# RoPE on one NeuronCore: whole batch rows in bf16, cast inside GpSimd-queue DMAs

## The chip, the core and the metric

The kernel runs on one NeuronCore of a Trainium2 chip. The metric is the device time of one execution in microseconds (us). Before the change the median of 10 executions is 318.76 us (318.5 to 323.6).

The core has engines that work side by side: VectorE (DVE in the profile), ScalarE (ACT), GpSimd (POOL), TensorE (PE, not used here) and SyncE (SP, used here only to issue transfers). Data lie in DRAM and are moved by 16 DMA engines into SBUF, which has 128 partitions, and back. A transfer is issued on the queue of the engine that issues it: SP's, ACT's or POOL's.

## The reference

Rotary position embedding on interleaved pairs: in each head, elements 2i and 2i+1 form a pair, which is rotated by an angle that depends on the position in the sequence and on i.

```python
x  # (8, 2048, 16, 64) float32: batch, position, head, element of the head
cos, sin  # (2048, 32) float32
x1, x2 = x_pairs[..., 0], x_pairs[..., 1]
out1 = x1 * cos - x2 * sin
out2 = x1 * sin + x2 * cos
out = np.stack([out1, out2], axis=-1)  # back to (8, 2048, 16, 64), float32
```

x has 67.1 MB and so has the output. The two tables have 0.26 MB each.

## The kernel before

One position is 16 heads x 64 elements = 1024 float32, 4 KB. The kernel cuts the sequence into G = 2 halves of 1024 positions; in each half a partition holds K = 8 consecutive positions. A tile `xt` is one half of one batch: 128 partitions x 8 positions, 32 KB a partition, 4 MB, and contiguous in DRAM in rows of 32 KB. There are 16 such tiles, and NX = 5 buffers for them.

A tile is worked on in pieces of 4 positions (4096 elements a partition). The first tile is cut into 1, 1, 2 and 4 positions, the last into 4, 2, 1 and 1, so that work begins and ends on small pieces. For each piece:

- `halve` (L75): ScalarE casts the piece from float32 to a bf16 buffer `xh`, of which there are three.
- `rotate`: VectorE does three tensor_tensor instructions in bf16. L94 multiplies by the sine table into `qt`, L95 multiplies in place by the cosine table, and L100 adds `qt` with the elements of each pair swapped. The swap is a matter of addressing. The sign of the first sine of each pair is put into the table.
- `widen` (L105): ScalarE casts the result back to float32, over the tile's own place. Then ACT's queue gets the store (L109): one for a tile, four for the last tile. After a tile's last piece SP's queue gets the load of the tile five further on (L70), which takes the same buffer and waits for its store.

The order is written out by hand (`manual_schedule`). SP issues the first tile's four pieces, the two tables (L115, L116), then four more tiles. VectorE makes bf16 tables from the float32 ones (L121 to L123). In the loop over pieces, ScalarE casts the next piece in before VectorE rotates this one, and then casts this one out.

Of the kernel before, what the change touches and what calls it, by code (L numbers as in the profile page):

```python
# [2 lines left out]

# [4 lines left out]


@with_exitstack  # L10
def kernel(
    ctx: ExitStack,
    tc: tile.TileContext,
    x: bass.AP,
    cos: bass.AP,
    sin: bass.AP,
    out: bass.AP,
):
    nc = tc.nc
    fp32 = mybir.dt.float32  # L20
    bf16 = mybir.dt.bfloat16
    mult = mybir.AluOpType.mult
    add = mybir.AluOpType.add

    B, S, H, D = x.shape
    P = 128
    K = 8
    G = S // (P * K)
    D2 = D // 2
    HD = H * D  # L30
    NX = 5


    x_t = x.rearrange("b (g p k) h d -> b g p k (h d)", p=P, k=K)
    out_t = out.rearrange("b (g p k) h d -> b g p k (h d)", p=P, k=K)
    cos_t = cos.rearrange("(g p k) c -> p g (k c)", p=P, k=K)
    sin_t = sin.rearrange("(g p k) c -> p g (k c)", p=P, k=K)

    consts = ctx.enter_context(tc.tile_pool(name="consts", bufs=1))
    xpool = ctx.enter_context(tc.tile_pool(name="xpool", bufs=NX))  # L40
    hpool = ctx.enter_context(tc.tile_pool(name="hpool", bufs=1))

    cos_sb = consts.tile([P, G, K * D2], fp32)
    sin_sb = consts.tile([P, G, K * D2], fp32)
    c_tab = consts.tile([P, G, K, D], bf16)
    s_tab = consts.tile([P, G, K, D], bf16)

    groups = [(g, b) for g in range(G) for b in range(B)]
    n = len(groups)
    first_runs = [(0, 1), (1, 2), (2, 4), (4, 8)]  # L50
    last_runs = [(0, 4), (4, 6), (6, 7), (7, 8)]

    def load_runs(i):
        return first_runs if i == 0 else last_runs if i == n - 1 else [(0, K)]

    def store_runs(i):
        return last_runs if i == n - 1 else [(0, K)]


    pieces = []  # L60
    for i in range(n):
        runs = first_runs if i == 0 else last_runs if i == n - 1 else [(0, 4), (4, 8)]
        pieces += [(i, k0, k1) for k0, k1 in runs]
    tiles, halved, rotated = {}, {}, {}

    def load(i):
        g, b = groups[i]
        tiles[i] = xpool.tile([P, K, HD], fp32, name="xt")
        for k0, k1 in load_runs(i):
            nc.sync.dma_start(out=tiles[i][:, k0:k1], in_=x_t[b, g, :, k0:k1])  # L70

    def halve(j):
        i, k0, k1 = pieces[j]
        halved[j] = hpool.tile([P, 4, HD], bf16, name="xh", bufs=3)
        nc.scalar.copy(out=halved[j][:, : k1 - k0], in_=tiles[i][:, k0:k1])  # L75

    def rotate(j):
        i, k0, k1 = pieces[j]
        g, _ = groups[i]
        nk = k1 - k0  # L80
        xh = halved.pop(j)
        qt = hpool.tile([P, 4, HD], bf16, name="qt")

        def rows(a):
            return a[:, :nk].rearrange("p k (h e) -> p k h e", h=H, e=D)

        def tab(a):
            return dataclasses.replace(
                a,
                offset=a.offset + (g * K + k0) * D,  # L90
                ap=[a.ap[0], [D, nk], [0, H], [1, D]],
            )

        nc.vector.tensor_tensor(out=rows(qt), in0=rows(xh), in1=tab(s_tab), op=mult)  # L94
        nc.vector.tensor_tensor(out=rows(xh), in0=rows(xh), in1=tab(c_tab), op=mult)  # L95
        q_swap = dataclasses.replace(
            qt, offset=qt.offset + 1, ap=[qt.ap[0], [2, nk * HD // 2], [-1, 2]]
        )
        xh3 = xh[:, :nk].rearrange("p k (a j) -> p (k a) j", j=2)
        nc.vector.tensor_tensor(out=xh3, in0=xh3, in1=q_swap, op=add)  # L100
        rotated[j] = xh

    def widen(j):
        i, k0, k1 = pieces[j]
        nc.scalar.copy(out=tiles[i][:, k0:k1], in_=rotated.pop(j)[:, : k1 - k0])  # L105
        g, b = groups[i]
        for r0, r1 in store_runs(i):
            if r1 == k1:
                nc.scalar.dma_start(out=out_t[b, g, :, r0:r1], in_=tiles[i][:, r0:r1])  # L109
        if k1 == K and i + NX < n:  # L110
            load(i + NX)

    with tc.manual_schedule():
        load(0)
        nc.sync.dma_start(out=cos_sb, in_=cos_t)  # L115
        nc.sync.dma_start(out=sin_sb, in_=sin_t)  # L116
        for i in range(1, NX):
            load(i)
        s2 = s_tab.rearrange("p g k (i j) -> p (g k i) j", j=2)
        sin_flat = sin_sb.rearrange("p g c -> p (g c)")  # L120
        nc.vector.tensor_copy(out=s2[:, :, 0], in_=sin_flat)  # L121
        nc.vector.tensor_scalar_mul(s2[:, :, 1], sin_flat, -1.0)  # L122
        nc.vector.tensor_copy(  # L123
            out=c_tab.rearrange("p g k (i j) -> p (g k i) j", j=2),
            in_=cos_sb.rearrange("p g c -> p (g c)").to_broadcast([P, G * K * D2, 2]),
        )
        halve(0)
        for j in range(len(pieces)):
            if j + 1 < len(pieces):
                halve(j + 1)  # L130
            rotate(j)
            widen(j)


# [1 line left out]
_INS = ['x', 'cos', 'sin']  # L136
_OUTS = [((8, 2048, 16, 64), 'float32')]


# [23 lines left out]
```

## Time and profile before

| | us |
|---|---|
| median of 10 executions | 318.76 |
| the profiled execution | 318.48 |
| its span in the trace | 316.7 |
| ScalarE, 30 casts in of 128x4096, each | 3.604 |
| ScalarE, 30 casts out of 128x4096, each | 3.602 |
| VectorE, 90 tensor_tensor of 128x4096, each | 2.292 |
| VectorE, tensor_tensor of 128x1024, each | 0.69 |
| median time from issue to landing, 4 MB load | 26.6 |
| median time from issue to landing, 4 MB store | 38.3 |

The span runs from the first to the last thing in the trace; 1.8 us of the profiled execution lie outside of it. An engine's busy time is the sum of its instructions; issuing a DMA does not count. The time from issue to landing contains the time in which a transfer stood behind others. The DMA row of the slices shows how busy the 16 DMA engines were on average, in tenths, and the row below it what they moved.

### The profile page before, as it was taken

The page shows a single profiled execution, that of the slowest core. Times are in us where ns is not written, and L with a number is a line of the kernel's source. Part 1 is how long each engine was busy: PE and PEld are TensorE (multiplying, and loading weights), DVE is VectorE, ACT ScalarE, POOL GpSimd, SP SyncE. Part 2 cuts the span into 40 slices and gives each one's busy share as a digit, 9 for nine tenths or more (in the row PEclk, how much of TensorE's full clock was granted, in tenths as well). Part 3 has the DMA queues.
Part 4 walks back from the last instruction along what each step waited for, and adds up shares of the span by engine and source line. Part 5 has one row for each costly group of instructions (what it writes and reads, how often), then busy time and mean ns, then how long its engine had stood idle before and what let it go on. Part 6 is the DMA issues. An engine that isn't in the chain of part 4 may idle for free.

```text
span 316.7 us, 352 instructions
## 1 busy us (share of the span) xinstructions
DVE 223.2 (70%) x111; ACT 230.0 (73%) x73; POOL 0.2 (0%) x4
## 2 busy tenths in 40 slices
DVE  0189999999999596693957939488440999999112
ACT  4078899999998693976949679495804999997322
POOL 0000000000000000000000000000000000000000
DMA  7999999999999999999999999999999999999997
GB/s 306 422 464 397 464 397 435 426 455 406 464 397 464 397 460 406 455 426 436 447 414 455 410 455 406 455 406 459 410 451 439 422 426 430 424 430 445 442 414 302
DMA packets 6450, 134.76 MB, mean 426 GB/s; under 512 B 688, under 2 KB 1200, under 8 KB 1968
## 3 DMA queue, kind: packets, MB, share of 16 engines
q1 hardware_dynamic: 3712, 67.63, 50.0%
q10 hardware_dynamic: 2736, 67.11, 49.1%
q14 instruction: 2, 0.02, 0.0%
HBM read 67.63 MB, written 67.11 MB: 425 GB/s over the span
## 4 chain that ended last, share of the span: by engine, by line
DMA 72%; ACT 16%; DVE 4%; issue 3%; another core or an unknown queue 2%; SPq 1%; ACTq 0%
DMA out_dram<-xt 38%; DMA xt<-in_x_dram 31%; ACT xt L105 9%; ACT xh L75 7%; DMA sin_sb<-in_sin_dram 4%; DVE xh L95 1%; DVE xh L100 1%; DVE qt L94 1%; SPq L70 1%; ACTq L109 0%; DVE s_tab L121 0%; SPq L115 0%; DVE s_tab L122 0%; DVE c_tab L123 0%
## 5 line engine op out<-in xcount | busy, mean ns | idle before, releaser
L75 ACT CAST xh<-xt 128x4096 bf16<-128x4096 f32 (+2 forms) x36 | 116.1, 3224 | 66.7 <-DMA xt<-in_x_dram 61.3
L105 ACT CAST xt<-xh 128x4096 f32<-128x4096 bf16 (+2 forms) x36 | 116.0, 3223 | 14.7 <-DVE xh L100 14.4
L94 DVE TENSOR_TENSOR qt<-xh,s_tab 128x4096 bf16<-128x4096 bf16 (+2 forms) x36 | 74.0, 2055 | 70.9 <-ACT xh L75 70.0
L95 DVE TENSOR_TENSOR xh<-xh,c_tab 128x4096 bf16<-128x4096 bf16 (+2 forms) x36 | 74.0, 2055 | 1.2
L100 DVE TENSOR_TENSOR xh<-xh,qt 128x4096 bf16<-128x4096 bf16 (+2 forms) x36 | 74.0, 2055 | 1.2
L121 DVE CAST s_tab<-sin_sb 128x512 bf16<-128x512 f32 x1 | 0.5, 453 | 14.5 <-DMA sin_sb<-in_sin_dram 14.5
L75 ACT ACT_TABLE_LOAD x1 | 1.3, 1283 | 0.7 <-PEq L147 0.7
L123 DVE CAST c_tab<-cos_sb 128x1024 bf16<-128x1024 f32 x1 | 0.7, 683 | 0.0
L122 DVE TENSOR_SCALAR s_tab<-sin_sb 128x512 bf16<-128x512 f32 x1 | 0.4, 441 | 0.0
L147 POOL MEMSET const-bfloat16-1.0<- 128x1 bf16 x1 | 0.1, 102 | 0.0
L147 POOL MEMSET const-uint8-127<- 128x1 uint8 x1 | 0.1, 102 | 0.0
L147 POOL MEMSET const-float32-0.0<- 128x1 f32 x1 | 0.1, 99 | 0.2 <-issue 0.2
L147 POOL MEMSET const-float32-1.0<- 128x1 f32 x1 | 0.1, 99 | 0.0
## 6 DMA issues: line engine op xcount, KB each, us to landing
out_dram<-xt ACTq DMA_DIRECT2D x15, 4096.0 KB, 38.3
xt<-in_x_dram SPq DMA_DIRECT2D x14, 4096.0 KB, 26.6
xt<-in_x_dram SPq DMA_DIRECT2D x2, 2048.0 KB, 16.4
xt<-in_x_dram SPq DMA_DIRECT2D x4, 512.0 KB, 24.2
xt<-in_x_dram SPq DMA_DIRECT2D x2, 1024.0 KB, 20.0
out_dram<-xt ACTq DMA_DIRECT2D x1, 2048.0 KB, 17.6
out_dram<-xt ACTq DMA_DIRECT2D x1, 1024.0 KB, 11.7
out_dram<-xt ACTq DMA_DIRECT2D x2, 512.0 KB, 4.1
```

Source lines behind the costliest of these rows:

```text
L70: nc.sync.dma_start(out=tiles[i][:, k0:k1], in_=x_t[b, g, :, k0:k1])
L75: nc.scalar.copy(out=halved[j][:, : k1 - k0], in_=tiles[i][:, k0:k1])
L94: nc.vector.tensor_tensor(out=rows(qt), in0=rows(xh), in1=tab(s_tab), op=mult)
L95: nc.vector.tensor_tensor(out=rows(xh), in0=rows(xh), in1=tab(c_tab), op=mult)
L100: nc.vector.tensor_tensor(out=xh3, in0=xh3, in1=q_swap, op=add)
L105: nc.scalar.copy(out=tiles[i][:, k0:k1], in_=rotated.pop(j)[:, : k1 - k0])
L121: nc.vector.tensor_copy(out=s2[:, :, 0], in_=sin_flat)
L122: nc.vector.tensor_scalar_mul(s2[:, :, 1], sin_flat, -1.0)
L123: nc.vector.tensor_copy(out=c_tab.rearrange("p g k (i j) -> p (g k i) j", j=2), in_=cos_sb.rearrange("p g c -> p (g c)").to_broadcast([P, ...
L147: nc = _bacc.Bacc("TRN2", target_bir_lowering=False, num_devices=1)
```

## The change

A tile becomes a whole batch row: 128 partitions x 16 positions. It lies in SBUF as bf16 (32 KB a partition), and in DRAM as rows of 64 KB. There are 8 tiles and again 5 buffers. The cast is part of the transfer: loads (L56) and stores (L59) are issued on GpSimd's queue with float32 on one side and bf16 on the other.

The first two positions of the first tile (1 MB) come in float32 through SP's queue into a staging tile (L85), and ScalarE casts them (L91). The last four positions of the last tile (2 MB) are cast by ScalarE into the same staging tile and go out in float32 through SP's queue (L121). A copy of one element (L119), which writes into the tile before the last, stands ahead of that cast and waits until that tile has been stored.

VectorE works in place in the tile, on 8 positions at a time (8192 elements a partition), in the first tile on 2, 6 and 8. These are 17 pieces of three instructions.

GpSimd's queue has this order: load 0 (14 positions), load 1, the store of the first two positions once they are rotated, loads 2, 3 and 4, the store of the rest of tile 0, store 1, load 5, store 2, load 6, store 3, load 7, stores 4, 5 and 6, and the store of the first twelve positions of tile 7. Loads 5, 6 and 7 wait until the tile whose buffer they take has been stored. A store waits for VectorE's work on its positions.

```diff
--- before.py
+++ after.py
@@ -24,112 +24,101 @@
     B, S, H, D = x.shape
     P = 128
-    K = 8
-    G = S // (P * K)
+    K = S // P
+    KP = 8
     D2 = D // 2
     HD = H * D
     NX = 5
+    HEAD = 2
+    TAIL = 4
-    x_t = x.rearrange("b (g p k) h d -> b g p k (h d)", p=P, k=K)
-    out_t = out.rearrange("b (g p k) h d -> b g p k (h d)", p=P, k=K)
-    cos_t = cos.rearrange("(g p k) c -> p g (k c)", p=P, k=K)
-    sin_t = sin.rearrange("(g p k) c -> p g (k c)", p=P, k=K)
+    x_t = x.rearrange("b (p k) h d -> b p k (h d)", p=P, k=K)
+    out_t = out.rearrange("b (p k) h d -> b p k (h d)", p=P, k=K)
+    cos_t = cos.rearrange("(p k) c -> p (k c)", p=P, k=K)
+    sin_t = sin.rearrange("(p k) c -> p (k c)", p=P, k=K)
     consts = ctx.enter_context(tc.tile_pool(name="consts", bufs=1))
     xpool = ctx.enter_context(tc.tile_pool(name="xpool", bufs=NX))
-    hpool = ctx.enter_context(tc.tile_pool(name="hpool", bufs=1))
+    qpool = ctx.enter_context(tc.tile_pool(name="qpool", bufs=1))
+    stage = ctx.enter_context(tc.tile_pool(name="stage", bufs=1))
-    cos_sb = consts.tile([P, G, K * D2], fp32)
-    sin_sb = consts.tile([P, G, K * D2], fp32)
-    c_tab = consts.tile([P, G, K, D], bf16)
-    s_tab = consts.tile([P, G, K, D], bf16)
+    cos_sb = consts.tile([P, K * D2], fp32)
+    sin_sb = consts.tile([P, K * D2], fp32)
+    c_tab = consts.tile([P, K, D], bf16)
+    s_tab = consts.tile([P, K, D], bf16)
-    groups = [(g, b) for g in range(G) for b in range(B)]
-    n = len(groups)
-    first_runs = [(0, 1), (1, 2), (2, 4), (4, 8)]
-    last_runs = [(0, 4), (4, 6), (6, 7), (7, 8)]
+    tiles = {}
-    def load_runs(i):
-        return first_runs if i == 0 else last_runs if i == n - 1 else [(0, K)]
+    def load(b, k0=0):
+        if b not in tiles:
+            tiles[b] = xpool.tile([P, K, HD], bf16, name="xt")
+        nc.gpsimd.dma_start(out=tiles[b][:, k0:], in_=x_t[b, :, k0:])
-    def store_runs(i):
-        return last_runs if i == n - 1 else [(0, K)]
+    def store(b, k0=0, k1=K):
+        nc.gpsimd.dma_start(out=out_t[b, :, k0:k1], in_=tiles[b][:, k0:k1])
-    pieces = []
-    for i in range(n):
-        runs = first_runs if i == 0 else last_runs if i == n - 1 else [(0, 4), (4, 8)]
-        pieces += [(i, k0, k1) for k0, k1 in runs]
-    tiles, halved, rotated = {}, {}, {}
-    def load(i):
-        g, b = groups[i]
-        tiles[i] = xpool.tile([P, K, HD], fp32, name="xt")
-        for k0, k1 in load_runs(i):
-            nc.sync.dma_start(out=tiles[i][:, k0:k1], in_=x_t[b, g, :, k0:k1])
-    def halve(j):
-        i, k0, k1 = pieces[j]
-        halved[j] = hpool.tile([P, 4, HD], bf16, name="xh", bufs=3)
-        nc.scalar.copy(out=halved[j][:, : k1 - k0], in_=tiles[i][:, k0:k1])
-    def rotate(j):
-        i, k0, k1 = pieces[j]
-        g, _ = groups[i]
+    def rotate(b, k0, k1):
         nk = k1 - k0
-        xh = halved.pop(j)
-        qt = hpool.tile([P, 4, HD], bf16, name="qt")
+        xp = tiles[b][:, k0:k1]
+        qt = qpool.tile([P, KP, HD], bf16, name="qt")
         def rows(a):
-            return a[:, :nk].rearrange("p k (h e) -> p k h e", h=H, e=D)
+            return a.rearrange("p k (h e) -> p k h e", h=H, e=D)
         def tab(a):
             return dataclasses.replace(
-                a,
-                offset=a.offset + (g * K + k0) * D,
-                ap=[a.ap[0], [D, nk], [0, H], [1, D]],
+                a, offset=a.offset + k0 * D, ap=[a.ap[0], [D, nk], [0, H], [1, D]]
             )
-        nc.vector.tensor_tensor(out=rows(qt), in0=rows(xh), in1=tab(s_tab), op=mult)
-        nc.vector.tensor_tensor(out=rows(xh), in0=rows(xh), in1=tab(c_tab), op=mult)
+        nc.vector.tensor_tensor(out=rows(qt[:, :nk]), in0=rows(xp), in1=tab(s_tab), op=mult)
+        nc.vector.tensor_tensor(out=rows(xp), in0=rows(xp), in1=tab(c_tab), op=mult)
         q_swap = dataclasses.replace(
             qt, offset=qt.offset + 1, ap=[qt.ap[0], [2, nk * HD // 2], [-1, 2]]
         )
-        xh3 = xh[:, :nk].rearrange("p k (a j) -> p (k a) j", j=2)
-        nc.vector.tensor_tensor(out=xh3, in0=xh3, in1=q_swap, op=add)
-        rotated[j] = xh
-    def widen(j):
-        i, k0, k1 = pieces[j]
-        nc.scalar.copy(out=tiles[i][:, k0:k1], in_=rotated.pop(j)[:, : k1 - k0])
-        g, b = groups[i]
-        for r0, r1 in store_runs(i):
-            if r1 == k1:
-                nc.scalar.dma_start(out=out_t[b, g, :, r0:r1], in_=tiles[i][:, r0:r1])
-        if k1 == K and i + NX < n:
-            load(i + NX)
+        x3 = xp.rearrange("p k (a j) -> p (k a) j", j=2)
+        nc.vector.tensor_tensor(out=x3, in0=x3, in1=q_swap, op=add)
     with tc.manual_schedule():
-        load(0)
+        head = stage.tile([P, TAIL, HD], fp32, name="st")
+        for k in range(HEAD):
+            nc.sync.dma_start(out=head[:, k : k + 1], in_=x_t[0, :, k : k + 1])
         nc.sync.dma_start(out=cos_sb, in_=cos_t)
         nc.sync.dma_start(out=sin_sb, in_=sin_t)
-        for i in range(1, NX):
-            load(i)
-        s2 = s_tab.rearrange("p g k (i j) -> p (g k i) j", j=2)
-        sin_flat = sin_sb.rearrange("p g c -> p (g c)")
-        nc.vector.tensor_copy(out=s2[:, :, 0], in_=sin_flat)
-        nc.vector.tensor_scalar_mul(s2[:, :, 1], sin_flat, -1.0)
+        load(0, HEAD)
+        load(1)
+        nc.scalar.copy(out=tiles[0][:, :HEAD], in_=head[:, :HEAD])
+        s2 = s_tab.rearrange("p k (i j) -> p (k i) j", j=2)
+        nc.vector.tensor_copy(out=s2[:, :, 0], in_=sin_sb)
+        nc.vector.tensor_scalar_mul(s2[:, :, 1], sin_sb, -1.0)
         nc.vector.tensor_copy(
-            out=c_tab.rearrange("p g k (i j) -> p (g k i) j", j=2),
-            in_=cos_sb.rearrange("p g c -> p (g c)").to_broadcast([P, G * K * D2, 2]),
+            out=c_tab.rearrange("p k (i j) -> p (k i) j", j=2),
+            in_=cos_sb.to_broadcast([P, K * D2, 2]),
         )
-        halve(0)
-        for j in range(len(pieces)):
-            if j + 1 < len(pieces):
-                halve(j + 1)
-            rotate(j)
-            widen(j)
+        for b in range(B):
+            if b == 0:
+                rotate(b, 0, HEAD)
+                store(b, 0, HEAD)
+                for c in range(2, NX):
+                    load(c)
+                rotate(b, HEAD, KP)
+            for k0 in range(KP if b == 0 else 0, K, KP):
+                rotate(b, k0, k0 + KP)
+            if b < B - 1:
+                store(b, HEAD if b == 0 else 0)
+            if b >= 1 and b - 1 + NX < B:
+                load(b - 1 + NX)
+        store(B - 1, 0, K - TAIL)
+        tail = stage.tile([P, TAIL, HD], fp32, name="st")
+        nc.scalar.copy(out=tiles[B - 2][:1, 0, :1], in_=tiles[B - 1][:1, K - 1, :1])
+        nc.scalar.copy(out=tail, in_=tiles[B - 1][:, K - TAIL :])
+        nc.sync.dma_start(out=out_t[B - 1, :, K - TAIL :], in_=tail)
 # ---- launch: one core; inputs and outputs as the reference has them ----
```

## The prediction

> **What bounds the kernel now.** I read the page's engine shares and its slices first, then the queue list, then the windows query for the rate stage by stage, and last the timeline of the end.
>
> ```profile
> span 316.7 us, 352 instructions
> DVE 223.2 (70%) x111; ACT 230.0 (73%) x73; POOL 0.2 (0%) x4
> DMA  7999999999999999999999999999999999999997
> DMA packets 6450, 134.76 MB, mean 426 GB/s; under 512 B 688, under 2 KB 1200, under 8 KB 1968
> q1 hardware_dynamic: 3712, 67.63, 50.0%
> q10 hardware_dynamic: 2736, 67.11, 49.1%
> ```
>
> Neither compute engine reaches three quarters of the span, and the DMA row is full in every slice but the first and the last. The loads (q1) and the stores (q10) together take 99.1% of sixteen engines' time. So the bound is bytes through the DMA engines, and a stage is worth what it adds to those bytes or to the gaps between them. The windows, with columns span, DVE, ACT, POOL, clock, DMA share and GB/s:
>
> ```profile
> 0.00:3.00 3.00, 0.00 (x0) 1.28 (x1) 0.20 (x4) 1.00 0.36 91
> 24.00:30.00 6.00, 5.25 (x3) 6.00 (x3) 0.00 (x0) 1.00 1.01 437
> 40.00:60.00 20.00, 18.90 (x9) 19.54 (x7) 0.00 (x0) 1.00 0.97 419
> 120.00:160.00 40.00, 28.08 (x13) 28.70 (x9) 0.00 (x0) 1.00 1.00 433
> 302.00:306.00 4.00, 0.00 (x0) 0.00 (x0) 0.00 (x0) 1.00 0.85 361
> 314.00:316.70 2.70, 0.00 (x0) 0.00 (x0) 0.00 (x0) 1.00 0.26 106
> ```
>
> From 24 to 30 us only loads run (the first store is issued at 36 us): 437 GB/s. From 120 to 160 us loads and stores share the engines: 433. That mixing opposite directions brings nothing says that an engine has one budget for both. At the start 3.00 us x (1 - 91/437) = 2.4 us are lost, at the end 2.70 x (1 - 106/433) = 2.0 us; the dips at 40 to 60 us (14/433 x 20 = 0.6) and 302 to 306 us (72/433 x 4 = 0.7) are what else a better order could save.
>
> How two queues share an engine is seen at the end, where the last load comes in one-position pieces (4 KB rows) beside stores with rows of 32 and 16 KB:
>
> ```profile
> 298.78 1.04 ACT L75 CAST xh<-xt 128x1024 bf16<-128x1024 f32 x1 [5.53 <-DMA xt<-in_x_dram]
> 307.88 1.04 ACT L75 CAST xh<-xt 128x1024 bf16<-128x1024 f32 x1 [6.26 <-DMA xt<-in_x_dram]
> ```
>
> The last 0.52 MB needs 9.1 us, 58 GB/s of some 430: the queue with short rows gets about one row per row of the other queue, not half of the bytes.
>
> **What the Trainium skill says.** "DMA: Bandwidth & Descriptors", section "SWDGE vs HWDGE vs iDMA": a cast during a transfer has to be issued from GpSimd, whose cores write the descriptors into rings in SBUF. The trace of before has no such transfer. Same page, "Queues, rings and completion order": each engine goes round its queues packet by packet; the 58 GB/s above agrees. Same page, "Latency and other measured facts": engines 7 and 15 are usually slower, with the GpSimd queue's rings as its best guess at the cause; before uses only hardware queues, so no run here shows it. "SBUF — State Buffer", section "Who interferes with whom": tensor_tensor takes the shared read interface only, so it should not hold up descriptor writing (the page calls this inferred); not shown here either.
>
> **The change part by part.**
>
> *The two casts on ScalarE go.* 36 + 36 casts, 116.1 + 116.0 us of ACT. What stays is one head cast of 2048 elements (1.90 us, the same shape's row), a table load of 1.28, a one-element copy and a tail cast of 4096 (3.60): about 7 us. On the path they were worth nothing except at the ends, since the DMA never ran dry in the middle.
>
> *VectorE.* Rows of 1024, 2048 and 4096 elements take 692, 1226 and 2292 ns, so 0.52 ns an element more; 8192 elements come to 2292 + 4096 x 0.52 = 4424 ns, 6144 to 3358. Fourteen pieces of eight positions, 14 x 3 x 4.424 = 185.8; one of six, 10.1; one of two, 3.7; the table instructions 1.6: sum 201.2 us against 223.2. These 22 us lie beside the DMA. Cover: tile b is rotated 26.5 us after tile b-1. With load 0 landed at about 22 us, tiles 0, 2, 4 and 7 are done near 45, 98, 151 and 231 us (tile 7 needs its load, below). At 19.4 us a tile (8.39 MB at 433) the queue reaches their stores near 104, 162, 240 and 300 us. More than 50 us of slack; VectorE would have to be a quarter slower to matter.
>
> *Queue order on GpSimd.* One queue carries load 0 (14 positions), load 1, store of the first two positions, loads 2 to 4, store 0, store 1, load 5, store 2, load 6, store 3, load 7, stores 4 to 7. A load waits for the store of the tile whose buffer it takes, and everything later on GpSimd waits behind it. Each time the store just issued is still to move 19.4 us of data, against a completion latency of some 2 us (last issue at 312.2, end at 316.7 for 0.5 MB), so I charge nothing; if that cover were gone, it would cost a gap of 2 to 3 us for each of the three waiting loads. The first store is different: loads 2 to 4 stand behind it, and it waits for VectorE. Loads 0 and 1 with head and tables are 17.3 MB, ending near 2.4 + 39.6 = 42 us; if the tables land before about 35 us, nothing is lost. See the rivals.
>
> *Bytes.* 67.11 MB in and 67.11 MB out on the DRAM side are unchanged, tables 0.52: 134.74 MB. On the SBUF side bf16 halves them for all but 3.1 MB. Which side the engine's time follows is not shown in before, since all its transfers are as wide on both sides. Bounds: the wide side, 0% gain; the narrow side, half of the time. I take the wide side: a load still has to bring in four bytes an element and a store to send out four, and since a mixture of directions gained nothing over one, I see no idle half that a narrower far side would free.
>
> *The rate of the casting queue.* Bounds: 437 (nothing lost, the loads-only window) and, for loss, no limit by any reason in the profile. The nearest price is the skill's own table for GpSimd-issued loads, same DMA page, section "Bandwidth", "Measured", which lists 425 GB/s for 16 MB; I use its rate column alone. I take 425 for the loads and this trace's 433 for the stores, for which there is no such figure.
>
> Sum: GpSimd loads 66.06 MB / 425 = 155.4 us. All else, 68.68 MB / 433 = 158.6. Start 2.4 (SP's first issue comes at 0.73 us as before). End 2.0. Two queues finishing within a row of each other at the end, and the switch into the software queue: 0.5, an estimate from the dips of 0.6 and 0.7 above. Span 318.9. The profiled execution took 318.48 with a span of 316.7, so 1.8 lie around it, and the median of the ten runs is 0.3 above that execution: 318.9 + 1.8 + 0.3 = 321.0.
>
> *The tail.* The one-element copy on ScalarE waits for the store of tile 6, then the 3.6 us cast, then SP issues 2.1 MB with 16 KB rows. At that time about 6 us of the 14.5 us of the GpSimd store (48 KB rows) are gone; row by row the two end within about 2 us of each other and the engines stay full. Nothing added.
>
> **The rivals.**
>
> 1. *The cast costs nothing: faster.* All 134.74 MB at 435, between the two windows: 309.7 + 2.4 + 2.0 + 0.5 = 314.6, and 316.7 as a median. For it: 131 MB in rows of 48 to 64 KB are at least as long as before, and the dips at 40 and 302 us have no counterpart. Against: it needs a software queue equal to a hardware one; the deciding rate is 430 GB/s, 1.6% below the loads-only window.
> 2. *The start starves: slower.* If GpSimd rows go as packets of 56 and 64 KB, there are 16 per engine in loads 0 and 1, against 32 of SP (8 each for two head pieces, cosines and sines). Row by row, the head lasts as long as both loads and the tables come after 42 us. Then 2 us to land, 1.3 of table work, 3 x 1.23 of rotation, about 1 to issue: near 8 us of empty engines before loads 2 to 4, 7.5 with what overlaps. That is rival 1 plus 7.5, 324.2. For it: the 58 GB/s at the end of before. Against: SP starts first, and if rows are cut to 32 KB or less the tables are in by 31 us and it costs nothing.
> 3. *The cast itself runs at a lower rate, or one engine lags.* Every engine carries its own rows, so one engine 5% slow ends 15 us late: 335; a rate of 380 gives 134.74/380 = 354.6, in all about 361. Nothing in before speaks for or against it.
> 4. *The narrow side counts.* Then 16 tiles need about 155 us of DMA and VectorE is the bound: tile 0 from 22 us, 201 - 5 = 196 us of rotation, then the last store and tail, 8.4 MB at up to 433, 10 to 19 us, and 4: about 240. For it: only that before cannot exclude it.
>
> **How the numbers follow.** The forecast, a small loss of rate, 0.38; rival 1, 0.25; rival 2, 0.12; rival 3, 0.13; rival 4 and anything partly like it, 0.07; a loss and a saving that cancel, 0.05. This kernel's runs can tell about 0.2% (0.6 us) from no change. Faster: 0.25 + 0.07 = 0.32; same: 0.05 and a little of the forecast's lower edge, 0.07; slower 0.61. Since both signs are there, the forecast's own range is 319 to 327 (rates of 433 to 421 with the same ends). The range for eight in ten takes in rival 1 at 437 (313 to 315) and rival 2, and goes into rival 3 as far as one lagging engine: 312 to 338, leaving out rival 4 and the worse half of rival 3.
>
> **What would show it.** The changed kernel's windows with loads alone (about 10 to 35 us) should show about 425 GB/s counted in DRAM bytes, and the stores-only end 433; VectorE near 201 us busy and ScalarE near 7; the 8192-element rows at 4.42 us; SP's head landed by 10 us and the first store issued before 40. A hole in the DMA row near 42 us would be rival 2. Full slices with a rate of 437 would be rival 1. DMA shares below full with VectorE busy without gaps would be rival 4. A DMA share full at a rate below 410, or a queue time that differs among engines, would be rival 3. What makes the prediction wrong is above all the rate: each 1% of it is 3.1 us.

## The result and the profile after

The changed kernel takes 326.42 us (median of 8, 326.3 to 327.2) against 318.69 before: a ratio of 1.0244, 95% interval 1.0235 to 1.0253. It is 7.7 us slower. The prediction had 321.0, so the sign was right and the size was a third of what came. That the sign was right was luck: the reason given for it, a slower casting queue, did not come.

From the page of the changed kernel: span, slices of DMA use, packets, queues (q0, the software queue, is GpSimd's, and q1, a hardware queue, is SP's), and the row of the first table instruction (busy and mean, then idle time before it and what ended that).

```profile
span 324.7 us, 153 instructions
DMA  9999919899899999999899999999999999999996
DMA packets 3169, 101.72 MB, mean 313 GB/s; under 512 B 352, under 2 KB 352, under 8 KB 864
q0 software_dynamic: 2448, 98.04, 94.6%
q1 hardware_dynamic: 720, 3.67, 3.1%
HBM read 67.63 MB, written 67.11 MB: 415 GB/s over the span
L93 DVE CAST s_tab<-sin_sb 128x512 bf16<-128x512 f32 x1 | 0.5, 454 | 44.0 <-DMA sin_sb<-in_sin_dram 44.0
```

The DMA row has one slice with a 1, the sixth (40.6 to 48.7 us). The last line says that VectorE's first instruction waited 44.0 us for the sine table, a transfer of 0.26 MB. In the kernel before, the same wait was 14.5 us:

```profile
L121 DVE CAST s_tab<-sin_sb 128x512 bf16<-128x512 f32 x1 | 0.5, 453 | 14.5 <-DMA sin_sb<-in_sin_dram 14.5
```

Two things about the byte counts: a casting load is booked with what it writes, bf16, so 101.72 MB stand where 134.76 stood; the HBM line has both directions in DRAM bytes. And of q0's 2448 packets, 17 transfers x 16 are completions, packets of 4 bytes that report a transfer's end on each engine; the 2176 others are 17 x 128, one packet for each partition's row, up to 64 KB long.

The windows around the hole (span, DVE, ACT, POOL, clock, DMA share, GB/s):

```profile
36.00:42.00 6.00, 0.00 (x0) 0.00 (x0) 0.00 (x0) 1.00 0.84 186
42.00:48.00 6.00, 3.93 (x6) 0.00 (x0) 0.00 (x0) 1.00 0.02 5
48.00:60.00 12.00, 11.86 (x5) 0.00 (x0) 2.13 (x4) 1.00 0.88 218
```

From 42 to 48 us the DMA engines have next to nothing to do, while VectorE works. By the trace's records of single rows, the last row before the hole ends at 43.5 us and the next begins at 50.7: 7.2 us. The timeline of the same stretch says why (start, length, engine, line, what; in brackets the idle time before):

```profile
2.10 0.43 SPq L87 DMA_DIRECT2D sin_sb<-in_sin_dram  x1
...
44.01 0.45 DVE L93 CAST s_tab<-sin_sb 128x512 bf16<-128x512 f32 x1 [44.01 <-DMA sin_sb<-in_sin_dram]
...
47.80 1.23 DVE L80 TENSOR_TENSOR xt<-xt,qt 128x2048 bf16<-128x2048 bf16 x1
...
49.59 0.54 POOL L59 DMA_DIRECT2D out_dram<-xt  x1 [47.14 <-DVE xt L80]
50.12 1.60 POOL L56 DMA_DIRECT2D xt<-in_x_dram  x3
```

The sines are issued at 2.1 us and land at 44.0, when loads 0 and 1 are through. VectorE makes its tables and rotates two positions until 49.0. GpSimd has stood for 47.14 us before the store of those two positions, and loads 2, 3 and 4 stand behind it on the same queue. Nothing is left to move until they have been issued.

The landing times of the SP transfers at the start (KB each, us from issue to landing) show a pattern:

```profile
st<-in_x_dram SPq DMA_DIRECT2D x2, 512.0 KB, 4.4
cos_sb<-in_cos_dram SPq DMA_DIRECT2D x1, 256.0 KB, 22.2
sin_sb<-in_sin_dram SPq DMA_DIRECT2D x1, 256.0 KB, 41.9
```

The head lands soon. Each table has 8 rows of 2 KB on each DMA engine. Load 0 also has 8 rows an engine, of 56 KB, and load 1 has 8 of 64 KB. The cosines land with the end of load 0, the sines with the end of load 1: one short row for one long row.

### The profile page after: what moved, and what is told of

It is laid out like the page before. It is cut to its first block, busy times and chain, and to the rows that moved or that the text cites. A ratio compares the mean times of both kernels' runs of the same rounds, so it can differ in the third digit from the quotient of the medians.

```text
span 324.7 us, 153 instructions
## 1 busy us (share of the span) xinstructions
DVE 214.2 (66%) x54; ACT 6.9 (2%) x4; POOL 9.4 (3%) x21
## 2 busy tenths in 40 slices
DMA packets 3169, 101.72 MB, mean 313 GB/s; under 512 B 352, under 2 KB 352, under 8 KB 864
## 3 DMA queue, kind: packets, MB, share of 16 engines
q0 software_dynamic: 2448, 98.04, 94.6%
## 4 chain that ended last, share of the span: by engine, by line
another core or an unknown queue 91%; DMA 2%; ACTq 1%; ACT 1%; SPq 0%; issue 0%
DMA st<-in_x_dram 2%; ACTq L147 1%; ACT xt L91 1%; ACT L91 0%; SPq L85 0%; ACT xt L119 0%; ACTq L119 0%; ACTq L91 0%
## 5 line engine op out<-in xcount | busy, mean ns | idle before, releaser
L74 DVE TENSOR_TENSOR qt<-xt,s_tab 128x8192 bf16<-128x8192 bf16 (+2 forms) x17 | 71.0, 4174 | 13.7 <-DMA xt<-in_x_dram 13.3
L80 DVE TENSOR_TENSOR xt<-xt,qt 128x8192 bf16<-128x8192 bf16 (+2 forms) x17 | 71.0, 4175 | 0.6
L75 DVE TENSOR_TENSOR xt<-xt,c_tab 128x8192 bf16<-128x8192 bf16 (+2 forms) x17 | 71.0, 4174 | 0.6
L59 POOL DMA_DIRECT2D out_dram<-xt x9 | 4.8, 535 | 179.7 <-DVE xt L80 179.7
L56 POOL DMA_DIRECT2D xt<-in_x_dram x8 | 4.4, 558 | 84.5 <-DMA out_dram<-xt 83.7
L119 ACT COPY xt<-xt 1x1 bf16<-1x1 bf16 x1 | 0.2, 193 | 295.3 <-DMA out_dram<-xt 295.3
L120 ACT CAST st<-xt 128x4096 f32<-128x4096 bf16 x1 | 3.6, 3598 | 0.0
L91 ACT CAST xt<-st 128x2048 bf16<-128x2048 f32 x1 | 1.9, 1897 | 0.0
## 6 DMA issues: line engine op xcount, KB each, us to landing
cos_sb<-in_cos_dram SPq DMA_DIRECT2D x1, 256.0 KB, 22.2
```

What stands on the lines that cost most here:

```text
L56: nc.gpsimd.dma_start(out=tiles[b][:, k0:], in_=x_t[b, :, k0:])
L59: nc.gpsimd.dma_start(out=out_t[b, :, k0:k1], in_=tiles[b][:, k0:k1])
L74: nc.vector.tensor_tensor(out=rows(qt[:, :nk]), in0=rows(xp), in1=tab(s_tab), op=mult)
L75: nc.vector.tensor_tensor(out=rows(xp), in0=rows(xp), in1=tab(c_tab), op=mult)
L80: nc.vector.tensor_tensor(out=x3, in0=x3, in1=q_swap, op=add)
L91: nc.scalar.copy(out=tiles[0][:, :HEAD], in_=head[:, :HEAD])
```

## The experiments

Theory A is the hole: the whole loss is the stretch without transfers, made by the starved table and the store that holds back three loads. Its rivals are B, a slower rate of the casting queue, and C, a gap that would only move.

**e1_loads_first.** Loads 2 to 4 go ahead of the store.

```diff
         load(0, HEAD)
-        load(1)
+        for c in range(1, NX):
+            load(c)
...
                 store(b, 0, HEAD)
-                for c in range(2, NX):
-                    load(c)
```

> The changed kernel with loads 2, 3 and 4 issued right behind load 1, ahead of the store of the first two positions. Theory A (the hole): the 7.6 us in which the engines are empty, from about 42 to 50 us, are the whole loss, because those three loads stood behind a store that waited for a late sine table. Then the median falls to 318.8 us (326.4 - 7.6), the table still lands near 44 us or later, and VectorE still starts late without any cost. Theory B (the rate): the casting queue moves bytes more slowly, and the hole only replaces waiting that would come anyway; then the time stays within 1 us of 326.4. Theory C (the hole moves): the loads' waits for buffers turn into a gap later; then about 322 to 326, with a new hole after 100 us.

Measured: 317.64 us, ratio to before 0.9961 (0.9948 to 0.9975). That is 8.8 us below the changed kernel, and 1.05 below the kernel before. The window of the hole in this run:

```profile
42.00:48.00 6.00, 3.72 (x5) 0.00 (x0) 0.00 (x0) 1.00 1.06 229
```

The sines still land 42.1 us after issue, VectorE still begins at 44.2 us, and it costs nothing. B and C fall as the cause: the same bytes through the same queue, and the loss is gone without a gap elsewhere. More came back than the 7.6 us that I had expected. Between the two profiled executions (326.44 and 318.12 us) the difference is 8.3 us, and 7.2 of them are the stretch without a row. About one microsecond beside it is not traced.

**e5_longer_wait and e6_longer_wait_loads_first.** The dose: five instead of one first multiplication for the first two positions, in the changed kernel and in e1.

```diff
-        nc.vector.tensor_tensor(out=rows(qt[:, :nk]), in0=rows(xp), in1=tab(s_tab), op=mult)
+        for _ in range(5 if (b, k0) == (0, 0) else 1):
+            nc.vector.tensor_tensor(out=rows(qt[:, :nk]), in0=rows(xp), in1=tab(s_tab), op=mult)
```

> The changed kernel with the first multiplication of the first two positions done five times instead of once (it writes the same values each time): four more instructions of 1.22 us in VectorE, 5.0 us with the gaps between them, right before the store that holds back loads 2 to 4. Theory A (the hole is set by tables, rotation and issue, in a chain): every microsecond ahead of that store is a microsecond of the end, 326.4 + 5.0 = 331.4 us, and the hole ends at about 55.5 instead of 50.5 us. Theory B (rate, VectorE has slack): nothing, 326.4.

> The same four instructions more in the kernel with loads 2 to 4 ahead of the store. Theory A: the queue is full to about 100 us, so 5.0 us more in VectorE cost nothing, 317.6 us within 0.5. If VectorE's late start had itself become the limit there, 322.6.

Measured: 331.59 us and 317.36 us. In the changed kernel 5.0 us of VectorE cost 5.2 us; with the loads first they cost nothing. The windows and the timeline of e5:

```profile
42.00:54.00 12.00, 9.77 (x10) 0.00 (x0) 0.00 (x0) 1.00 0.01 3
...
54.65 0.54 POOL L59 DMA_DIRECT2D out_dram<-xt  x1 [52.20 <-DVE xt L81]
```

The store moved from 49.59 to 54.65 us, and the empty stretch grew with it.

**e2_tables_first.** The tables change places with the head on SP's queue.

```diff
+        nc.sync.dma_start(out=cos_sb, in_=cos_t)
+        nc.sync.dma_start(out=sin_sb, in_=sin_t)
         for k in range(HEAD):
             nc.sync.dma_start(out=head[:, k : k + 1], in_=x_t[0, :, k : k + 1])
-        nc.sync.dma_start(out=cos_sb, in_=cos_t)
-        nc.sync.dma_start(out=sin_sb, in_=sin_t)
```

> The changed kernel with the two tables issued on SP's queue ahead of the two head pieces; GpSimd's order as in the changed kernel. Theory A: a queue gets one row for each row of the other. The tables (16 rows an engine) are through before GpSimd's rows start, at about 5 to 7 us; of the head's rows some 8 an engine are left, which go row by row beside 56 KB rows of 2.1 us each and land near 22 to 25 us. The first store is issued near 30 us, before the loads run out near 42, no hole, 318.8 us. Theory B: no change, 326.4. If queues shared by bytes, the head would be starved less or more than that but not by whole rows: landing below 12 us or beyond 40.

Measured: 328.91 us, 2.5 us more than the changed kernel. (Between the profiled executions it is 1.6 us, as much as the first store goes out later: 51.15 us against 49.59.) The expectation failed. The tables did land early (the first table instruction starts at 4.05 us), but now the head is starved. The times from issue to landing of the tile `st` (the smallest is the tail's store):

```profile
DMA to landing us min/median/max: 15.5/23.2/41.4
```

The two head pieces landed 23.2 and 41.4 us after issue; the tables in the same two places had needed 22.2 and 41.9. A head piece has twice the bytes of a table, but the same 8 rows an engine. So a queue's share does not go by bytes. Every transfer here has 8 rows an engine, so that these times alone would also fit turns by whole transfers. The packets of the changed kernel from 26 to 36 us, in the middle of load 1, decide it (queue: packets, MB, share of the engines):

```profile
q0 software_dynamic: 64, 2.10, 97.2%
q1 hardware_dynamic: 64, 0.13, 3.8%
```

There are 64 rows of the sines beside 64 rows of the load. With turns by transfers, the sines' 128 rows would stand together at one point. The turns go row by row.

My error was in how many rows SP gets through first: I had counted some 24 an engine, it was the 16 of the two transfers issued before GpSimd's first, in both kernels.

**e3_short_rows.** Loads 0 and 1 are cut into transfers of four positions.

```diff
-        nc.gpsimd.dma_start(out=tiles[b][:, k0:], in_=x_t[b, :, k0:])
+        step = 4 if b < 2 else K
+        for k in range(k0, K, step):
+            k1 = min(k + step, K)
+            nc.gpsimd.dma_start(out=tiles[b][:, k:k1], in_=x_t[b, :, k:k1])
```

> The changed kernel with loads 0 and 1 cut into transfers of four positions (rows of 16 KB, in load 0 a last one of 8 KB), nothing else moved. Theory A, row by row: the 16 table rows an engine alternate with rows of 0.6 us instead of 2.1 and 2.4 us, so the cosines land near 10 us and the sines near 15 instead of 24 and 44; no hole; 318.8 us, plus up to 0.5 for shorter rows. If queues shared by bytes, the length of the other queue's rows would not matter: the sines land near 44 us again and the time stays at 326.4. Theory B: 326.4 or a little more.

Measured: 317.79 us, ratio 0.9968 (0.9955 to 0.998). GpSimd's order is that of the changed kernel; only loads 0 and 1 became more transfers with shorter rows:

```profile
cos_sb<-in_cos_dram SPq DMA_DIRECT2D x1, 256.0 KB, 10.3
sin_sb<-in_sin_dram SPq DMA_DIRECT2D x1, 256.0 KB, 15.5
```

Sixteen rows of 0.6 us instead of 2.1 and 2.4, and the tables come as expected. With the same bytes ahead and beside, the length of the other queue's rows sets the landing time.

**e10_sines_on_act.** The sine table is issued on ScalarE's idle queue.

```diff
-        nc.sync.dma_start(out=sin_sb, in_=sin_t)
+        nc.scalar.dma_start(out=sin_sb, in_=sin_t)
```

> The changed kernel with the sine table issued on ScalarE's queue, which is idle at the start, instead of last on SP's. Theory A: the sines are ahead of GpSimd's rows (below 8 us); the cosines are third on SP as before, 8 rows an engine beside 56 KB rows, near 24 us; VectorE starts there, the first store goes out near 30 us, before loads 0 and 1 are through, no hole: 317.6 us within 0.6, without any change in GpSimd's order. Theory B: 326.4.

Measured: 317.9 us, ratio 0.9972 (0.9964 to 0.9979). One word repairs the kernel. The sines are used at 5.3 us, and the store is out before loads 0 and 1 end:

```profile
5.31 0.45 DVE L93 CAST s_tab<-sin_sb 128x512 bf16<-128x512 f32 x1 [5.31 <-DMA sin_sb<-in_sin_dram]
...
30.77 0.69 DVE L95 CAST c_tab<-cos_sb 128x1024 bf16<-128x1024 f32 x1 [24.67 <-DMA cos_sb<-in_cos_dram]
...
35.69 0.54 POOL L59 DMA_DIRECT2D out_dram<-xt  x1 [33.24 <-DVE xt L80]
```

The cosines came at 30.8 us, not at 24. With the sines taking turns with the head on the engines, the head's second piece was still unfinished when GpSimd's rows began (it landed at 12.3 us), and its last rows stood ahead of the cosines. The cosines' landing in the middle of load 1 (30.8 us) fits turns by rows again, not by transfers.

**e7_rows_32k and e8_pool_only.** What the other parts of the change are worth, both measured on e1: in e7 each GpSimd transfer is cut in two at position 8, and in e8 there is no float32 head and tail (the lines with `head`, `tail` and the copies at L91, L119, L120 left out, `load(0)` and `store(B - 1)` whole). The diff is that of e7.

```diff
-        nc.gpsimd.dma_start(out=tiles[b][:, k0:], in_=x_t[b, :, k0:])
+        for k, k1 in ((k0, KP), (KP, K)):
+            nc.gpsimd.dma_start(out=tiles[b][:, k:k1], in_=x_t[b, :, k:k1])
...
-        nc.gpsimd.dma_start(out=out_t[b, :, k0:k1], in_=tiles[b][:, k0:k1])
+        for r0, r1 in ((k0, min(k1, KP)), (KP, k1)):
+            if r0 < r1:
+                nc.gpsimd.dma_start(out=out_t[b, :, r0:r1], in_=tiles[b][:, r0:r1])
```

> The kernel with loads 2 to 4 first, every GpSimd load and store cut into two transfers at position 8, so that rows in DRAM are 32 KB instead of 64 (24 KB and less in the first and last tile). It measures what the 64 KB rows are worth. Theory A: a row has a fixed cost of about 10 to 25 ns beside its bytes, on 16 more rows a tile and engine (8 each way) and 8 tiles, 128 rows x 0.02 = some 2 to 3 us more: 319.5 to 320.5, and the sines land earlier, near 27 us. If row length does not matter at this size, 317.6 within 0.5.

> The kernel with loads 2 to 4 first, without the float32 head and tail: all of x and the output go through GpSimd's casting queue, only the tables go over SP, issued first. It measures what head and tail over SP are worth. Theory A: the flow is the same, its start moves from SP's issue at 0.74 to GpSimd's at 1.25 us, filled in part by the tables, so 0 to 0.8 us more: 317.6 to 318.4 us; the tables land near 4 us, VectorE starts with load 0 near 22 us. If a store on the casting queue alone at the end ends late, up to 3 us more: 320.6.

Measured: 319.53 us with 32 KB rows, 318.71 us without head and tail. The long rows save 1.9 us. The edit also doubles the number of transfers, but the records of single rows point to the rows: a 64 KB row takes 2.432 us as a load and 2.449 as a store, two rows of 32 KB take 2 x 1.227 and 2 x 1.245. That is 22 and 41 ns for the second row, where the expectation had 10 to 25; over some sixty rows an engine each way it would come to 4 us, more than was measured. Head and tail over SP save 1.1 us by the median, but e8's 14 times lie in two groups, eight from 318.1 to 318.9 us and six from 319.3 to 320.0, so that the saving is about 0.7 or 2.2; why there are two is open. With 32 KB rows, the size of the kernel before, the casting queue is 0.8 us slower than that kernel (ratio 1.0024, 1.0014 to 1.0034). At that row length the cast in the transfer brought no time; the longer rows did.

**e4_soft_queue_fp32 and e9_soft_both_fp32.** The software queue without a cast, in the kernel before: loads alone on it, then loads and stores (there a load is issued one tile later).

```diff
-            nc.sync.dma_start(out=tiles[i][:, k0:k1], in_=x_t[b, g, :, k0:k1])
+            nc.gpsimd.dma_start(out=tiles[i][:, k0:k1], in_=x_t[b, g, :, k0:k1])
... (e9 as well:)
-                nc.scalar.dma_start(out=out_t[b, g, :, r0:r1], in_=tiles[i][:, r0:r1])
-        if k1 == K and i + NX < n:
-            load(i + NX)
+                nc.gpsimd.dma_start(out=out_t[b, g, :, r0:r1], in_=tiles[i][:, r0:r1])
+        if k1 == K and 0 <= i - 1 and i - 1 + NX < n:
+            load(i - 1 + NX)
```

> The kernel before with its loads issued on GpSimd's queue instead of SP's, in float32 without a cast; tables stay on SP, stores on ACT's queue. It measures the software queue without a cast. If the software queue costs rate as the prediction assumed for loads (425 GB/s against 433), 67 MB take 2.9 us longer: about 321.6 us. If the queue as such costs nothing, 318.7 within 0.6 us. In both cases the tables on SP may land late or early beside 32 KB rows, but no load waits behind VectorE here until the buffers run out.

> The kernel before with loads and stores in float32 on GpSimd's queue, no cast in any transfer, 32 KB rows; a load goes one tile later than its buffer's store, so that the wait for that store has another store to hide behind; tables on SP. It separates the software queue from the cast, and a lone software queue from one beside a hardware queue (the run with the loads alone on it took 326.1). If a software queue is slowed by a hardware queue at its side, the lone one runs at full rate: 318 to 320 us. If the software queue in float32 costs rate by itself, 324 us or more again.

Measured: 326.09 and 324.22 us. e4 fits neither branch. e9 lies where its second branch had it, but hardly because of a lower rate. The windows from 40 to 300 us of e4, of e9 and of the kernel before:

```profile
40.00:300.00 260.00, 188.97 (x83) 193.42 (x55) 7.36 (x14) 1.00 1.00 426
40.00:300.00 260.00, 197.55 (x92) 203.69 (x62) 16.93 (x32) 1.00 1.00 431
40.00:300.00 260.00, 196.35 (x88) 202.22 (x60) 0.00 (x0) 1.00 1.00 432
```

The ends of e4 and of e9:

```profile
316.00:324.60 8.60, 2.08 (x3) 3.04 (x3) 0.00 (x0) 1.00 0.45 186
316.00:323.20 7.20, 0.00 (x0) 0.00 (x0) 0.00 (x0) 1.00 0.15 63
```

In the middle, a software queue of loads beside a hardware queue of stores moves 426 GB/s; that is worth 3.6 us of e4's 7.4. With both on the software queue it is 431, and in the kernel before 432. At the end both run out slowly. e9 has no compute left there: from 315.5 to 318.5 us some six rows are under way at a time instead of sixteen (one for each engine). In e4 the last pieces also land late and are still computed on. In e1 sixteen rows are under way until 313.5 us, and the last ends at 315.1. Why the software queue in float32 ends unevenly was not settled. So these two runs don't price the software queue for the changed kernel; e1 does.

## Why the prediction was right or wrong

It was wrong in size, because it put the right mechanism among the rivals. Step by step:

- **The bound.** Right. Without the hole (e1) the DMA engines are full to the end, with ScalarE at 6.9 us and VectorE far from the path; the span is 316.4 us against 316.7 before.
- **The wide side counts.** Right. The narrow side would have given about 240 us; e1 with the same bytes in DRAM takes 317.6.
- **The queue order on GpSimd.** This is the step that failed: "if the tables land before about 35 us, nothing is lost", with the forecast resting on that. The cosines landed at 23.8 us, the sines at 44.0, and the first store was issued at 49.6 us, not before 40. The result is a hole of 7.2 us and a loss of 8.8, where the forecast had none. Rival 2 describes what came: tables after 42 us, then table work, a rotation and an issue, and an empty stretch. It stood at 0.12 because I took it that SP would start first and that GpSimd's rows might be cut. SP's first two transfers did come first, its last two did not, and no row was cut. (Rival 2 was not right throughout: it had the head land with the loads, and the head landed by 6.2 us.) The kernel before had already shown the sharing (58 GB/s for 4 KB rows); what I did not follow through was that the tables are last on SP's queue, and that 16 rows an engine of theirs meet just the 16 rows of loads 0 and 1.
- **The size of the hole.** Rival 2 had 324.2 us, 7.5 us on 316.7. Measured: 8.8 us on 317.6. Two of its parts were off in opposite directions: the sines were in use 0.5 us after their last row, where it had 2 us, and from the end of the rotation to the first new row it took 1.7 us, where it had 1. That the stretch came so close (7.2 us) is in part luck.
- **The rate.** Mis-sized the other way. In e1 a 64 KB load row takes 2.43 us on its engine, which is 431 GB/s on sixteen, and a store row 2.45 us, 428: the loads are not the slower side. The loads at 425 GB/s made the span without a hole 318.9, the run without the hole has 316.4; in medians 321.0 against 317.64. With the same 2.4 and 2.0 us lost at the ends, 134.74 MB in 312.0 us are 431.9 GB/s, where the forecast's mean was 429.1. In medians the two errors are 321.0 - 3.4 (rate and ends) + 8.8 (hole) = 326.4. They pulled in opposite directions, which made the miss smaller. Of the 3.4 us, 0.9 is no rate: the forecast added 2.1 us from span to median, and in e1 they lie 1.2 apart, since its profiled execution was the slowest of five.
- **The dips.** I took 419 GB/s at 40 to 60 us and 361 at 302 to 306 us for gaps that a better order could save. In short windows the trace books a row as a whole: in the changed kernel the window from 3 to 6 us has a DMA share of 1.45, the next 0.74. A dip beside a peak in windows of a few rows' length is no gap: in the kernel before, 446 GB/s follow the 419, and the 8 us around the other dip have 440.
- **VectorE.** I counted fourteen pieces of eight positions; there are fifteen (one in tile 0, two in each of the other seven). 15 x 3 x 4.425 us and the rest give 214 us, and the page has 214.2. The duration of 4424 ns was right to 2 ns, and the 13 us error cost nothing.
- **The tail and the loads' waits.** No gap after 60 us; charged at nothing, and nothing it was. GpSimd's 83.7 us of waiting for stores were all covered.
- **An engine that lags (rival 3).** It did not come: the last rows of e1 end within 1.6 us of each other.

Of the places in the Trainium skill: that engines go round their queues packet by packet ("DMA: Bandwidth & Descriptors", "Queues, rings and completion order") agrees with e2, e3 and the 64 rows beside 64. The page counts a packet in descriptors, typically 9 to 17; the trace has no descriptors, and what it shows is that each turn moved one row, of 2 KB or of 64. That tensor_tensor does not hold up descriptor writing ("SBUF — State Buffer", "Who interferes with whom") agrees: most of GpSimd's issues take 0.53 to 0.54 us each while VectorE is busy without a break, no longer than its first ones with VectorE idle (1.21 us for two).

## What to carry to other kernels

In these runs a transfer with short rows beside one with long rows got one row per row: its landing time was its number of rows on each engine times the other queue's row time, and its bytes hardly mattered. So issue small tables before the big transfers start, if need be on an idle queue (e2, e10), or keep the big rows short until the tables are in (e3). Count what then stands behind them: in e2 it was the head that starved. And when a store waits for a compute engine on an in-order queue, put every load that has its buffer already ahead of it; that cover made the late table free (e1, e6).

## What the runs showed that I had not expected

- Three edits that touch nothing in common (the order of three loads, the row length of two, the queue of one 0.26 MB table) each take off 8.5 to 8.8 us and end within 0.3 us of each other, at 317.64 to 317.9: the repaired kernel is about 0.3% faster than the kernel before.
- A float32 to bf16 transfer costs the time of its float32 side. A 64 KB row takes 2.43 us (load) or 2.45 (store), two plain rows of 32 KB in the kernel before 2 x 1.213: within 1%.
- The software queue in float32 ends unevenly: 7.2 us at 63 GB/s in e9. The cause is open.
